# Hybrid layer (HGRN2 beside MLA): rope step of the MLA queries cut in three and pinned in the engines' orders; token-sum tiles laid in another order

## The chip, the cores and the metric

The kernel runs on one core of one Trainium2 chip. A core has a matrix engine (TensorE, PE in the profile), VectorE (DVE), ScalarE (ACT), GpSimd (POOL) and SyncE (SP). Each engine carries out its own instructions in order and waits for the others through semaphores. ACT, POOL and SP also issue DMA transfers; an issue stands in the engine's order like any other instruction. The metric is the time of one execution on the device in microseconds (us), the median of several runs; lower is better.

## The reference

One decoder layer for 512 tokens of width 1024, in float32. A normed input h is projected to all the columns that two branches and their gates need:

```
h    = rms_norm(x);  proj = h @ w_in
hq, hf, hi, hz, cq, ckv, kr, mz, glog = split(proj)
y_a  = HGRN2(hq, hf, hi) per head, normed, * silu(hz)     # 8 heads of 128, a gated linear recurrence in chunks of 32
q    = rms_norm(cq) @ w_uq                                # 8 heads of 128 + 64
q_pe = rope(q[..., 128:])                                 # the 64 rope columns of each head
kv   = rms_norm(ckv) @ w_ukv;  k_pe = rope(kr)            # one rope key for all heads
y_b  = causal softmax((q_nope k_nope + q_pe k_pe) * scale) @ v, * silu(mz)
m    = sigmoid(g_a) * (y_a @ w_proj_a) + sigmoid(g_b) * (y_b @ w_proj_b)
out  = rms_norm(x + m @ w_out)
```

The change touches how and when `q_pe` is made, and where some operands of the gates' products lie in memory.

## The kernel before

Every large matrix product is done as three products of rounded parts (high by high, high by low, low by high): `mm3`, L91 to L93. The parts of the weights are made on the fly: ACT casts the high part `w_hi` (L118), DVE subtracts to get the low part `w_lo` (L119). The accumulators of projections lie in three PSUM slots called `mm_ps`; a slot is free for PE again when whoever reads it is done.

The program has four stages: the norm and the low-rank projections (to about 55 us), HGRN2 in four pairs of heads (`hg_pair`, to about 290 us), the eight MLA heads (to about 425 us), and the gates' and the output's products, in the manner of Strassen.

In `hg_pair` the order is: forget projection and `hg_forget` for two heads (ACT: tanh, L454; DVE: f L455, scan L459, reciprocal L460, then products; POOL: L456, L457, small products, and at the end k64, L477), then for odd pairs the gate (ACT L562, DVE L563, `z`), the query projection and `hg_query` (ACT L485, POOL L489 and others), `hg_states` (PE transposes L498, ACT copy kt L499, PE products L503), scores, and `hg_out` with its norm (ACT L547, POOL L165 and L166). Pair 3 is the last, and around it the first MLA head is started: `mla_turn(0)` stands in the program before pair 3, `mla_rope` and `mla_nope(0)` after its states.

The rope for a pair of MLA heads: `mla_turn` makes the rope columns of q by a small product, ACT copies them (L626), four DMAs issued by ACT swap the halves of each head (L628), POOL multiplies by the two tables and adds (L629 to L631, each 128x512), and two more DMAs issued by ACT swap the two heads (L635, 128 KB each). `mla_rope` then has ACT round the swapped part (qh, L641) and copy each head's own rows (qp, L644), and DVE subtract for the other rows (L645).

An MLA head has scores (`mla_scores`: PE, L691 being the rope part; DVE; ACT exp L697; POOL scaling of p, L699), then a gate, the next head's q and k (`mla_nope`, whose parts qn and kn are made by ACT L160 and DVE L161), the previous head's output, and the transposes of p (L715).

Where one engine's order isn't written out by hand, the scheduler orders an engine's instructions as it estimates that they are ready. `tc.issue_after(x)` pins instructions behind x in their own engine's order. `last_pool` holds the last computing instruction of a step on POOL; `step()` has POOL issue two adding DMAs (L758) behind it, one pair after each stage of a pair or head, to build weight sums in DRAM.

Tiles of a `Pool` are laid out by the order of allocation. After the MLA heads the pool `h_sums` takes tiles s1 to s4, into which POOL loads sums of the tokens (L949) that the gates' products use.

Of the kernel before, what the change touches and what calls it, by code (L numbers as in the profile page):

```python
# [9 lines left out]
F32 = mybir.dt.float32  # L10
F32R = mybir.dt.float32r
U8 = mybir.dt.uint8
BF16 = mybir.dt.bfloat16
AF = mybir.ActivationFunctionType
ALU = mybir.AluOpType
# [3 lines left out]
P = 128  # L19
D = 1024  # L20
S = 512
NT = S // P
KD = D // P
H = 8
# [8 lines left out]
SCALE = (128 + 64) ** -0.5  # L33
# [5 lines left out]
def hybrid_layer(ctx: ExitStack, tc: tile.TileContext, a):  # L39
    nc = tc.nc  # L40
# [19 lines left out]
    def z_tile():  # L60
        return zpool.tile([P, S], F32, tag="z", name="z")
# [91 lines left out]
            for t in range(2):  # L153
                done(2 * t2 + t, ps[t])

    last_pool = [None]

    def split(hi, lo, src):

# [268 lines left out]
    ma_pool = Pool("mla_a", "right")  # L428
    qtab = ma_pool.tile([P, 2, S], F32, "qtab")
# [5 lines left out]
    for i in range(2):  # L435
        gh = hw.tile([P, NT, 12], F32, f"gh{i}")
# [7 lines left out]
    c4 = lambda t: t[:].rearrange("p (g n c) -> p g n c", n=4, c=C)  # L444
    c2_ = lambda t: t[:].rearrange("p (g n c) -> p g n c", n=2, c=C)

    def bc(gh, o, n):
        return gh[:, :, o : o + n].rearrange("p g (n o) -> p g n o", o=1).broadcast_to([P, NT, n, C])
# [32 lines left out]
    def hg_query(h, pq, pr):  # L481

        gh = gh_[h % 2]
        q = W("f", 1)
        nc.scalar.activation(q[:], pq[:], AF.Tanh, scale=0.5)  # L485
        nc.vector.scalar_tensor_tensor(q[:], q[:], 1.0, pq[:], op0=ALU.add, op1=ALU.mult)
        qi, q128, q64 = W("qi"), W("q128"), W("q64", 2, (P, S // 2))
        nc.vector.tensor_tensor(qi[:], q[:], pr[:], op=ALU.mult)
        last_pool[0] = nc.gpsimd.tensor_tensor(c2_(q64), c4(qi)[:, :, 2:4], bc(gh, 10, 2), op=ALU.mult)  # L489
        nc.vector.tensor_tensor(c4(q128), c4(qi), bc(gh, 4, 4), op=ALU.mult)  # L490
        return qi, q64, q128

    def hg_states(h, k128, ft, v_sb):
# [70 lines left out]

    v_sb = [None] * NT

    def hg_pair(pair, before_gate=None, last=None):
        cc, hs = pair * 256, (2 * pair, 2 * pair + 1)
        pf = proj_ch(w_in, COL_F + cc, hT)
        kk = [hg_forget(h, pf[i]) for i, h in enumerate(hs)]  # L570
        if pair:
            step()
        else:
            early_sums(kh[0])
        def gate():
            pz = proj_ch(w_in, COL_ZA + cc, hT)
            zz = [z_tile() for _ in hs]
            for i in range(2):
                silu2(zz[i][:], pz[i][:])
            return zz  # L580

        if pair % 2 == 0:
            for t in range(NT):
                v_sb[t] = hw.tile([P, 512], F32, f"v{t}")
            proj_tok(w_in, COL_I + cc, hT, lambda t, ps: nc.scalar.copy(v_sb[t][:], ps[:]))
        else:
            zz = gate()
        pq = proj_ch(w_in, COL_Q + cc, hT)
        qq = [hg_query(h, pq[i], kk[i][0]) for i, h in enumerate(hs)]
        step()  # L590
        sts = [hg_states(h, kk[i][5], kk[i][1], v_sb) for i, h in enumerate(hs)]
        if before_gate:
            before_gate()
        if pair % 2 == 0:
            zz = gate()
        def scores():
            return hg_scores([(h, kk[i][2:5] + qq[i][0:2]) for i, h in enumerate(hs)])

        def outs(aa):
            on = [hg_out(h, aa[i], sts[i], qq[i][2], v_sb) for i, h in enumerate(hs)]  # L600
            step()
            return on

        def gated(on):
            for i, h in enumerate(hs):
                hg_gate(h, on[i], zz[i])

        if last:
            return last(scores, outs, gated)
        gated(outs(scores()))  # L610
# [11 lines left out]
    def mla_turn(pair):  # L622

        ps = low(load_w(w_uq[:, :, 2 * pair : 2 * pair + 2, 128:192]), 0, 3)
        qr, qs = ma_pool.tile([P, S], F32, "qr"), ma_pool.tile([P, S], F32, "qs")
        nc.scalar.copy(qr[:], ps[:])  # L626
        for b in range(4):
            nc.scalar.dma_start(qs[32 * b : 32 * b + 32, :], qr[32 * (b ^ 1) : 32 * (b ^ 1) + 32, :])  # L628
        nc.gpsimd.tensor_tensor(qr[:], qr[:], qtab[:, 0], op=ALU.mult)  # L629
        nc.gpsimd.tensor_tensor(qs[:], qs[:], qtab[:, 1], op=ALU.mult)  # L630
        nc.gpsimd.tensor_tensor(qr[:], qr[:], qs[:], op=ALU.add)  # L631

        qx = ma_pool.tile([P, S], F32, "qs")
        for i in range(2):
            nc.scalar.dma_start(qx[64 * i : 64 * i + 64, :], qr[64 - 64 * i : 128 - 64 * i, :])  # L635
        return qr, qx

    def mla_rope(qr, qx):

        qp, qh = [ma_pool.tile([P, S], F32R, f"qp{i}") for i in range(2)], ma_pool.tile([P, S], F32R, "qh")  # L640
        nc.scalar.copy(qh[:], qx[:])  # L641
        for i in range(2):
            own, other = slice(64 * i, 64 * i + 64), slice(64 - 64 * i, 128 - 64 * i)
            nc.scalar.copy(qp[i][own], qr[own])  # L644
            nc.vector.tensor_tensor(qp[i][other], qx[other], qh[other].bitcast(F32), op=ALU.subtract)  # L645
        return qp

    def mla_values(h0):
# [32 lines left out]
    def mla_scores(h, pool, qn, kn, qp, final=False):  # L681

        pn = []
        for i in range(NT):
            n = (i + 1) * P
            bl = slice(i * P, n)
            sps = ax_tile()
            qh = qp[h % 2]
            mm3(sps[:, :n], qn, kn, (slice(None), bl), (slice(None), slice(0, n)), True, False)
            for x in range(2):  # L690
                nc.tensor.matmul(sps[:, :n], qh[:, bl], kpe[x][:, :n], start=False, stop=x == 1)  # L691
            sm = pool.tile([P, 4], F32, "sm", 4)
            p = pool.tile([P, n], F32, f"p{i}")
            nc.vector.tensor_tensor(sps[:, bl], sps[:, bl], mask_inf[:], op=ALU.add)
            nc.vector.tensor_reduce(sm[:, 0:1], sps[:, :n], axis=AX.X, op=ALU.max, negate=True)
            nc.vector.tensor_scalar(sm[:, 1:2], sm[:, 0:1], SCALE, None, op0=ALU.mult)  # L696
            nc.scalar.activation(p[:, :n], sps[:, :n], AF.Exp, scale=SCALE, bias=sm[:, 1:2], accum_out=sm[:, 2:3])  # L697
            nc.vector.reciprocal(sm[:, 3:4], sm[:, 2:3])
            scaled_p = (nc.vector if final else nc.gpsimd).tensor_scalar(p[:, :n], p[:, :n], sm[:, 3:4], 0.5,  # L699
                                                                         op0=ALU.mult, op1=ALU.mult)  # L700
            if not final:
                last_pool[0] = scaled_p
            pn.append(p)
        return pn
# [98 lines left out]
    def step():  # L803
        if adds and last_pool[0]:
            x = adds.pop(0)
            if x:
                x[0].add(x[1])
# [20 lines left out]
            gated(on)  # L828
        return z

    turned_q = mla_turn(0)
    z = hg_pair(H // 2 - 1, first_scores, last_outputs)
    hw.close()

    def a_parts(src, to):
# [70 lines left out]
    yb = ybp.tile([P, H, S], F32, "yb")  # L906
    qp, nope, pn = early
    late = None
    for h in range(H):
        pools = (ma_pool, mw)  # L910
        if h % 2 and h + 1 < H:
            turned_q = mla_turn((h + 1) // 2)
        if h:
            pn = mla_scores(h, pools[h % 2], *nope, qp, h + 1 == H)
        if h % 2 and h + 1 < H:
            qp = mla_rope(*turned_q)
        if h:
            z = mla_gate(h)
        if h:
            if h + 1 < H:  # L920
                nope = mla_nope(h + 1, pools[(h + 1) % 2])
            mla_out(*late)
            if h % 4 == 0:
                v = mla_values(h)
        hook = lambda: mla_transpose(pn)
        if h + 1 == H:
            with tc.manual_schedule(engines={mybir.EngineType.PE}):
                pts, later = [], []
                w11, w21 = gate_w[0].block(0, 0), gate_w[0].block(1, 0)
                u = ch_product(w11, h11, copied("c11", 1.0))  # L930
                ch_product(w21, h12, lambda b, ps: later.append((b, ps)), tile=mm_tile, hook=lambda: pts.extend(hook()))
                mla_out(h, pts, v, z)
        elif h:
            late = (h, hook(), v, z)
            step()
        else:
            with tc.manual_schedule(engines={mybir.EngineType.PE}):
                nope = mla_nope(1, pools[1])
                v = mla_values(0)
                late = (0, hook(), v, z)  # L940
    mw.close()
    ma_pool.close()
    cpool.close()

    hs = Pool("h_sums", "right")
    s1, s2, s3, s4 = [[hs.tile([P, 4, 256], F32R, f"s{n}{i}") for i in range(2)] for n in range(1, 5)]
    for n, s in ((1, s1), (2, s2), (4, s4), (3, s3)):
        for i in range(2):
            nc.gpsimd.dma_start(s[i][:], h_dram[n - 1][i][:])  # L949
# [82 lines left out]
    s1, s2 = [[sp.tile([P, 4, 256], F32R, f"s{n}{i}") for i in range(2)] for n in (1, 2)]  # L1032
# [173 lines left out]
```

## Time and profile before

| | us |
|---|---|
| median of 3 runs (lowest to highest) | 622.16 (621.46 to 623.14) |
| the profiled execution, its own time | 623.33 |
| its span | 621.4 |
| PE busy in the span | 604.7 (97%) |
| DVE, ACT, POOL busy | 431.7, 285.2, 147.6 |

The rows are read so: in an order of time, the first two numbers are start and duration in us, then engine, line, operation, result and operands, and in brackets how long the engine stood idle before it and who ended that. In a list by line, "min/median/max" are durations in ns. In a window row the numbers are the length, PE's busy time with its count of products, the granted TensorE clock (1.00 is full), the DMA engines' busy share and GB/s.

### The profile page before, as it was taken

How to read it: one execution, taken by the hardware profiler on the slowest of the kernel's cores; microseconds unless marked ns; L12 is line 12 of the kernel's file. 1: busy time of each engine (PE TensorE's matmuls, PEld its weight loads, DVE VectorE, ACT ScalarE, POOL GpSimd, SP SyncE). 2: the span in 40 equal slices, each digit the busy share in tenths (PEclk: the TensorE clock that was granted, in tenths of full speed). 3: DMA queues.
4: the chain of work that ended last, by engine and by line, in shares of the span. 5: the costliest groups of instructions: out<-in, count | busy, mean ns of one | idle time of the engine just before them, and what ended most of it. 6: DMA issues, size and time to landing. Idle time of an engine off the chain costs nothing.

```text
span 621.4 us, 9796 instructions
## 1 busy us (share of the span) xinstructions
PE 604.7 (97%) x3688; PEld 528.3 (85%) x3688; DVE 431.7 (69%) x679; ACT 285.2 (46%) x531; POOL 147.6 (24%) x245
## 2 busy tenths in 40 slices
PE   8999999999999998999998999999999999999995
PEld 5998888888888886788887888799999999888884
DVE  7727989499864538948564864766865787676796
ACT  5645244323243342335553555446667764323452
POOL 3106322444350155411525223320000000000002
PEclk9999999999999998999999999999999999999998
DMA  8449479987979946572466577496656556595213
GB/s 272 142 143 334 156 225 374 289 213 166 286 130 297 246 131 126 115 142 70 98 127 140 120 164 174 86 326 196 191 186 202 181 172 193 184 339 188 69 34 136
DMA packets 74800, 114.37 MB, mean 184 GB/s; under 512 B 7513, under 2 KB 41727, under 8 KB 74753
## 3 DMA queue, kind: packets, MB, share of 16 engines
q1 hardware_dynamic: 65100, 89.69, 44.8%
q0 software_dynamic: 7952, 21.50, 19.2%
q10 hardware_dynamic: 1700, 2.56, 1.4%
q8 instruction: 29, 0.48, 0.3%
q14 instruction: 19, 0.15, 0.1%
HBM read 105.34 MB, written 39.85 MB: 234 GB/s over the span
## 4 chain that ended last, share of the span: by engine, by line
PE 69%; DVE 10%; DMA 8%; ACT 5%; issue 4%; POOL 2%; ACTq 1%; POOLq 0%; SPq 0%; DVEq 0%
PE ax_ps L849 16%; PE mm_ps L91 13%; PE mm_ps L92 13%; PE mm_ps L93 13%; PE mm_ps L849 3%; DVE w_lo L119 3%; DMA w_raw<-w_proj_b 2%; DMA w_raw<-w_uq 2%; ACT w_hi L118 2%; PE mm_ps L271 2%; DMA qs<-qr 1%; DMA w_raw<-out_t 1%; DMA w_raw<-w_out 1%; DVE ya L1077 1%; PE ax_ps L691 1%
## 5 line engine op out<-in xcount | busy, mean ns | idle before, releaser
L119 DVE TENSOR_TENSOR w_lo<-w_raw,w_hi 128x1024 fp32r<-128x1024 f32 (+3 forms) x116 | 136.7, 1190 | 98.5 <-ACT w_hi L118 92.8
L118 ACT CAST w_hi<-w_raw 128x1024 fp32r<-128x1024 f32 (+3 forms) x116 | 114.8, 1004 | 147.4 <-PE mm_ps L92 65.1
L91 PE MATMUL mm_ps<-hT,w_hi 128*128 128x512 f32 x320 | 126.3, 396 | 2.8 <-DVE z L563 2.0
L92 PE MATMUL mm_ps<-hT,w_hi 128*128 128x512 f32 x320 | 125.7, 393 | 0.0
L93 PE MATMUL mm_ps<-hT,w_lo 128*128 128x512 f32 x320 | 125.5, 394 | 0.0
L91 PEld LDWEIGHTS mm_ps<-hT,w_hi 128*128 128x128 f32 x320 | 60.6, 189 | 15.7 <-DVE z L563 2.4
L93 PEld LDWEIGHTS mm_ps<-hT,w_lo 128*128 128x128 f32 x320 | 60.5, 189 | 12.6
L92 PEld LDWEIGHTS mm_ps<-hT,w_hi 128*128 128x128 f32 x320 | 60.5, 189 | 11.9
L849 PE MATMUL ax_ps<-s,w_hi 128*128 128x256 f32 x384 | 54.1, 283 | 0.2 <-ACT w_hi L118 0.2
L849 PEld LDWEIGHTS ax_ps<-s,w_hi 128*128 128x128 f32 x384 | 49.6, 192 | 0.5 <-ACT w_hi L118 0.5
L1094 POOL TENSOR_SCALAR ssum<-ssum 128x1 f32<-128x1 f32 x3 | 0.9, 310 | 183.9 <-ACT sq L1081 183.9
L93 PE MATMUL mm_ps<-w_hi,hT 128*128 128x512 f32 (+1 forms) x96 | 36.6, 383 | 0.0
L92 PE MATMUL mm_ps<-w_lo,hT 128*128 128x512 f32 (+1 forms) x96 | 36.5, 382 | 0.0
L91 PE MATMUL mm_ps<-w_hi,hT 128*128 128x512 f32 (+1 forms) x96 | 36.4, 386 | 0.0
L849 PE MATMUL ax_ps<-s,w_lo 128*128 128x256 f32 x192 | 31.3, 284 | 0.2 <-DVE w_lo L119 0.2
L699 POOL TENSOR_SCALAR p<-p,sm 128x128 f32<-128x128 f32 (+3 forms) x28 | 15.8, 568 | 63.5 <-DVE sm L696 52.7
L697 ACT ACTIVATE p<-ax_ps,sm 128x128 f32<-128x128 f32 (+3 forms) x32 | 16.9, 530 | 26.1 <-DVE sm L696 23.9
L849 PEld LDWEIGHTS ax_ps<-s,w_lo 128*128 128x128 f32 x192 | 26.6, 192 | 0.4 <-DVE w_lo L119 0.4
L460 DVE RECIPROCAL tf<-pr 128x512 f32<-128x512 f32 x8 | 26.8, 3346 | 0.1
L457 POOL TENSOR_SCALAR k<-tf,c1n,c 128x512 f32<-128x512 f32 x8 | 16.0, 1995 | 26.6 <-ACT tf L454 26.6
L91 PE MATMUL mm_ps<-cT,w_hi 128*128 128x512 f32 x52 | 20.7, 398 | 0.0
L93 PEld LDWEIGHTS mm_ps<-w_hi,hT 128*128 128x128 f32 x96 | 18.0, 188 | 3.0
(298 smaller groups left out, 1210.9 us busy)
## 6 DMA issues: line engine op xcount, KB each, us to landing
w_raw<-w_in SPq DMA_DIRECT2D x54, 512.0 KB, 6.5
g_t<-w_in SPq DMA_DIRECT2D x16, 512.0 KB, 8.8
w_raw<-g_t SPq DMA_DIRECT2D x16, 512.0 KB, 4.8
g_t<-w_in POOLq DMA_DIRECT2D x8, 512.0 KB, 10.9
pa_t<-w_proj_a SPq DMA_DIRECT2D x8, 512.0 KB, 13.2
g_t<-g_t POOLq DMA_DIRECT2D x8, 512.0 KB, 11.3
out_t<-w_out SPq DMA_DIRECT2D x8, 512.0 KB, 8.8
s<-h POOLq DMA_DIRECT2D x8, 512.0 KB, 7.6
```

The source lines that it names most:

```text
L91: nc.tensor.matmul(ps, lh[lsl], rh[rsl], start=start, stop=False)
L92: nc.tensor.matmul(ps, lh[lsl], rl[rsl], start=False, stop=False)
L93: nc.tensor.matmul(ps, ll[lsl], rh[rsl], start=False, stop=stop)
L118: last_hi[0] = nc.scalar.copy(hi[:, :o], raw[:, :o])
L119: last_lo[0] = nc.vector.tensor_tensor(lo[:, :o], raw[:, :o], hi[:, :o].bitcast(F32), op=ALU.subtract)
L271: nc.tensor.matmul(ps, hT[l][:, 4 * kh + k, t * P : t * P + P], c_hl[kh][r][:, k * 256 : k * 256 + 256], start=kh == 0 and kind == 0 and k ...
L457: nc.gpsimd.tensor_scalar(k[:], tf[:], c1n[:, h : h + 1], c1[:, h : h + 1], op0=ALU.mult, op1=ALU.add)
L460: nc.vector.reciprocal(rp[:], pr[:])
L691: nc.tensor.matmul(sps[:, :n], qh[:, bl], kpe[x][:, :n], start=False, stop=x == 1)
L697: nc.scalar.activation(p[:, :n], sps[:, :n], AF.Exp, scale=SCALE, bias=sm[:, 1:2], accum_out=sm[:, 2:3])
L699: scaled_p = (nc.vector if final else nc.gpsimd).tensor_scalar(p[:, :n], p[:, :n], sm[:, 3:4], 0.5, op0=ALU.mult, op1=ALU.mult)
L849: nc.tensor.matmul(ps[:, o], w[k // 2][i][:, k % 2, cols], ap[j][:, k], start=not banks and c == 0 and n == 0, stop=n == 11, skip_group_ch ...
```

## The change

Three pieces take the place of two. `mla_turn` ends after the four half swaps. A new `mla_rotate` has the three POOL operations (now L636 to L638) and the two swaps of heads, which POOL now issues (L641); all of it is pinned behind `last_pool`, and becomes `last_pool` itself, so that a following `step()` comes after it. `mla_rope` (ACT L649 and L652, DVE L653) is pinned behind `last_act` and `last_dve`, which are set in `hg_query` and `mla_scores`. For pair 0 the rotation is called after pair 3's forget steps, `mla_rope` stays after its states. `mla_turn(1)` moves from head 1 to before head 0; the turns for pairs 2 and 3 go from heads 3 and 5 to heads 2 and 4, and the rotations follow heads 0, 2 and 4. In the pool `h_sums`, s3 is now laid first, then s1, s2, s4; the loads are issued in the order they had.

```diff
-    last_pool = [None]
+    last_pool, last_dve, last_act = [None], [None], [None]
...
-        nc.scalar.activation(q[:], pq[:], AF.Tanh, scale=0.5)
+        last_act[0] = nc.scalar.activation(q[:], pq[:], AF.Tanh, scale=0.5)
...
-        nc.vector.tensor_tensor(c4(q128), c4(qi), bc(gh, 4, 4), op=ALU.mult)
+        last_dve[0] = nc.vector.tensor_tensor(c4(q128), c4(qi), bc(gh, 4, 4), op=ALU.mult)
...
-    def hg_pair(pair, before_gate=None, last=None):
+    def hg_pair(pair, after_forget=None, before_gate=None, last=None):
...
         kk = [hg_forget(h, pf[i]) for i, h in enumerate(hs)]
+        if after_forget:
+            after_forget()
         if pair:
             step()
...
             nc.scalar.dma_start(qs[32 * b : 32 * b + 32, :], qr[32 * (b ^ 1) : 32 * (b ^ 1) + 32, :])
-        nc.gpsimd.tensor_tensor(qr[:], qr[:], qtab[:, 0], op=ALU.mult)
-        nc.gpsimd.tensor_tensor(qs[:], qs[:], qtab[:, 1], op=ALU.mult)
-        nc.gpsimd.tensor_tensor(qr[:], qr[:], qs[:], op=ALU.add)
-
-        qx = ma_pool.tile([P, S], F32, "qs")
-        for i in range(2):
-            nc.scalar.dma_start(qx[64 * i : 64 * i + 64, :], qr[64 - 64 * i : 128 - 64 * i, :])
+        return qr, qs
+
+    def mla_rotate(qr, qs):
+
+        with tc.issue_after(last_pool[0].ins):
+            nc.gpsimd.tensor_tensor(qr[:], qr[:], qtab[:, 0], op=ALU.mult)
+            nc.gpsimd.tensor_tensor(qs[:], qs[:], qtab[:, 1], op=ALU.mult)
+            nc.gpsimd.tensor_tensor(qr[:], qr[:], qs[:], op=ALU.add)
+            qx = ma_pool.tile([P, S], F32, "qs")
+            for i in range(2):
+                turn = nc.gpsimd.dma_start(qx[64 * i : 64 * i + 64, :], qr[64 - 64 * i : 128 - 64 * i, :])
+        last_pool[0] = turn
         return qr, qx
...
-        nc.scalar.copy(qh[:], qx[:])
-        for i in range(2):
-            own, other = slice(64 * i, 64 * i + 64), slice(64 - 64 * i, 128 - 64 * i)
-            nc.scalar.copy(qp[i][own], qr[own])
-            nc.vector.tensor_tensor(qp[i][other], qx[other], qh[other].bitcast(F32), op=ALU.subtract)
+        with tc.issue_after(last_act[0].ins), tc.issue_after(last_dve[0].ins):
+            nc.scalar.copy(qh[:], qx[:])
+            for i in range(2):
+                own, other = slice(64 * i, 64 * i + 64), slice(64 - 64 * i, 128 - 64 * i)
+                nc.scalar.copy(qp[i][own], qr[own])
+                nc.vector.tensor_tensor(qp[i][other], qx[other], qh[other].bitcast(F32), op=ALU.subtract)
         return qp
...
-            nc.scalar.activation(p[:, :n], sps[:, :n], AF.Exp, scale=SCALE, bias=sm[:, 1:2], accum_out=sm[:, 2:3])
-            nc.vector.reciprocal(sm[:, 3:4], sm[:, 2:3])
+            last_act[0] = nc.scalar.activation(p[:, :n], sps[:, :n], AF.Exp, scale=SCALE, bias=sm[:, 1:2], accum_out=sm[:, 2:3])
+            last_dve[0] = nc.vector.reciprocal(sm[:, 3:4], sm[:, 2:3])
...
-    turned_q = mla_turn(0)
-    z = hg_pair(H // 2 - 1, first_scores, last_outputs)
+    turned_q = list(mla_turn(0))
+
+    def rotate():
+        turned_q[:] = mla_rotate(*turned_q)
+
+    z = hg_pair(H // 2 - 1, rotate, first_scores, last_outputs)
...
+    turned_q = mla_turn(1)
     for h in range(H):
         pools = (ma_pool, mw)
-        if h % 2 and h + 1 < H:
-            turned_q = mla_turn((h + 1) // 2)
+        if h in (2, 4):
+            turned_q = mla_turn(h // 2 + 1)
...
             late = (h, hook(), v, z)
+            if h in (2, 4):
+                turned_q = mla_rotate(*turned_q)
             step()
...
+            turned_q = mla_rotate(*turned_q)
...
-    s1, s2, s3, s4 = [[hs.tile([P, 4, 256], F32R, f"s{n}{i}") for i in range(2)] for n in range(1, 5)]
+    s3, s1, s2, s4 = [[hs.tile([P, 4, 256], F32R, f"s{n}{i}") for i in range(2)] for n in (3, 1, 2, 4)]
```

How this moves instructions is shown at three places. The first is ACT in the forget part of pair 3, before (tf is the tanh of each of the two heads, qp and qh belong to the rope, the DMA is the swap of heads):

```order
L118 CAST w_hi<-w_raw 128x1024
L635 DMA qs<-qr 64x512 x2
L454 ACTIVATE tf<-mm_ps 128x512
L644 CAST qp_2574<-qr 64x512
L644 CAST qp_2575<-qr 64x512
L118 CAST w_hi<-w_raw 128x1024
L641 CAST qh<-qs 128x512
L118 CAST w_hi<-w_raw 128x640
L562 ACTIVATE z<-mm_ps 128x512
L454 ACTIVATE tf<-mm_ps 128x512
```

and now:

```order
L118 CAST w_hi<-w_raw 128x1024
L454 ACTIVATE tf<-mm_ps 128x512
L118 CAST w_hi<-w_raw 128x1024
L118 CAST w_hi<-w_raw 128x640
L454 ACTIVATE tf<-mm_ps 128x512
L562 ACTIVATE z<-mm_ps 128x512
```

The swap and the three rope casts have left this part, and the second tanh stands ahead of the gate's.

The second place is ACT at the states of pair 3, from the query's tanh (f) of the second head to the second head's kt; qn and kn are parts of MLA head 0. Before:

```order
L485 ACTIVATE f<-mm_ps 128x512
L499 COPY kt<-ax_ps 128x384
L160 CAST qn_2599<-mm_ps 128x512
L118 CAST w_hi<-w_raw 128x384
L160 CAST kn_2610<-mm_ps 128x512
L499 COPY kt<-ax_ps 128x384
```

and now:

```order
L485 ACTIVATE f<-mm_ps 128x512
L652 CAST qp_2574<-qr 64x512
L652 CAST qp_2575<-qr 64x512
L499 COPY kt<-ax_ps 128x384
L160 CAST qn_2599<-mm_ps 128x512
L118 CAST w_hi<-w_raw 128x1024
L160 CAST kn_2610<-mm_ps 128x512
L649 CAST qh<-qs 128x512
L499 COPY kt<-ax_ps 128x384
```

The rope casts stand ahead of the first kt, qh ahead of the second.

The third place is POOL in the same pair, from the second head's last key product (k) to the query products (q); g_t and pa_t are weight sums in DRAM, the numbers are those of buffers. Before:

```order
L477 TENSOR_TENSOR k_2385<-ko,gh_643 128x256
L758 DMA g_t_654<-g_t_652 128x1024 x2
L489 TENSOR_TENSOR q_2531<-qi,gh_639 128x256
L489 TENSOR_TENSOR q_2540<-qi,gh_643 128x256
L758 DMA pa_t_657<-w_proj_a 128x2x512 x2
```

and now:

```order
L477 TENSOR_TENSOR k_2379<-ko,gh_643 128x256
L636 TENSOR_TENSOR qr<-qr,qtab 128x512
L637 TENSOR_TENSOR qs<-qs,qtab 128x512
L638 TENSOR_TENSOR qr<-qr,qs 128x512
L489 TENSOR_TENSOR q_2531<-qi,gh_639 128x256
L641 DMA qs<-qr 64x512 x2
L766 DMA g_t_654<-g_t_652 128x1024 x2
L489 TENSOR_TENSOR q_2540<-qi,gh_643 128x256
L766 DMA pa_t_657<-w_proj_a 128x2x512 x2
```

Rotation and swap stand behind the last key product; before, the rotation stood ahead of the whole forget part.

## Prediction

> **What bounds the kernel now.** I read the page's head, then what TensorE (PE) waits for between 210 and 430 us (the only stretch in which the change moves work), then the windows and the order of time around each wait.
>
> ```profile
> span 621.4 us, 9796 instructions
> PE 604.7 (97%) x3688; PEld 528.3 (85%) x3688; DVE 431.7 (69%) x679; ACT 285.2 (46%) x531; POOL 147.6 (24%) x245
> ```
>
> PE is busy 604.7 of 621.4 us and the change takes no product away. It can only gain where PE stands still or runs at a lower clock. PE's waits from 210 to 430 us (us in total, times, longest):
>
> ```profile
> PE ax_ps L715 <- POOL p L699: 2.1, 2, 1.4
> PE mm_ps L91 <- DVE z L563: 2.0, 1, 2.0
> PE ax_ps L91 <- DVE pt L161: 1.0, 1, 1.0
> PE mm_ps L91 <- DVE qn L161: 0.8, 2, 0.5
> PE ax_ps L503 <- ACT kt L499: 0.6, 1, 0.6
> ```
>
> So 6.5 us in all is to be had, and what the clock loses behind a wait. The longest wait is in pair 3 (PE in order of time; then PE's busy time, the granted clock PEclk, DMA share and GB/s by windows):
>
> ```profile
> 244.25 0.50 PE L91 MATMUL mm_ps<-hT,w_hi 128*128 128x512 f32 x1 [1.99 <-DVE z L563]
> ...
> 245.06 0.40 PE L91 MATMUL mm_ps<-hT,w_hi 128*128 128x512 f32 x1
> 245.29 0.55 PE L92 MATMUL mm_ps<-hT,w_hi 128*128 128x512 f32 x1
> ...
> 248.62 0.48 PE L91 MATMUL mm_ps<-hT,w_hi 128*128 128x512 f32 x1
> ...
> 256.90 0.49 PE L498 MATMUL ax_ps<-ident,k 128*128 128x128 f32 x3
> ...
> 262.47 0.94 PE L503 MATMUL ax_ps<-v,kt 128*128 128x128 f32 x6 [0.62 <-ACT kt L499]
> ```
>
> ```profile
> 246.00:248.00 2.00, 2.00 (x6) 0.50 0.09 26
> ```
>
> ```profile
> 100.00:216.00 116.00, 116.00 (x769) 1.00 0.93 242
> 322.00:355.00 33.00, 30.58 (x159) 1.00 0.64 129
> ```
>
> A little over a microsecond after the 1.99 us wait the granted clock is 0.50: the eight products that start from 245.29 up to 248.62 take 3.33 us, where at the 0.23 before them (245.06 to 245.29) they would take 1.8. The wait costs 1.99 + 1.5 = 3.5 us. Pairs 1 and 2, which have the same forget steps and no rope beside them, run from 100 to 216 us without a pause.
>
> Why PE waits there: ScalarE (ACT), VectorE (DVE) and GpSimd (POOL) in order of time.
>
> ```profile
> 229.13 1.51 ACTq L635 DMA_DIRECT2D qs<-qr  x2
> 230.70 0.60 ACT L454 ACTIVATE tf<-mm_ps 128x512 f32<-128x512 f32 x1 [4.78 <-PE mm_ps L93]
> ...
> 243.69 0.60 ACT L454 ACTIVATE tf<-mm_ps 128x512 f32<-128x512 f32 x1 [3.51 <-DVE ki L475]
> ```
>
> ```profile
> 234.79 1.84 DVE L645 TENSOR_TENSOR qp<-qs,qh 64x512 fp32r<-64x512 f32 x2
> 236.56 1.21 DVE L459 TENSOR_TENSOR_SCAN pr<-f,fr 128x512 f32<-128x512 f32 x1
> ```
>
> ```profile
> 227.83 1.27 POOL L631 TENSOR_TENSOR qr<-qr,qs 128x512 f32<-128x512 f32 x1
> ```
>
> POOL's rope addition ends at 229.10. Until then the swap's two DMA issues sit at the head of ACT's queue, with the forget step's tanh (L454) behind them. On DVE the two rope subtractions end only at 236.63, and the scan of the same forget step follows at once. So scan, reciprocal, gate z, and the accumulator that z frees for PE, are all late.
>
> **Part 1: rope of pair 0 leaves pair 3's forget part.** ACT issue, rope casts and DVE subtractions move behind the query step. What is left is pair 1's order, which has no pause; I take the 3.5 us as gone. Next in line is nothing that the profile of pairs 1 and 2 shows. PE then reaches the transposes of the states (L498) at 256.90 - 3.5 = 253.4, and the second head's states product (L503), ready at 262.47 - 0.62 = 261.85, at 258.35.
>
> **Part 2: a new wait at the states.** ACT's new order there is: two rope casts qp (which wait for POOL's addition), kt of the first head, qn, a weight cast, kn, qh (which waits for the swap to land), kt of the second head. Behind qh, then, stands the copy that the second L503 needs. When does the swap land? The template is pair 1, ACT, POOL and PE:
>
> ```profile
> 120.35 0.60 ACT L454 ACTIVATE tf<-mm_ps 128x512 f32<-128x512 f32 x1 [1.34 <-PE mm_ps L93]
> ```
>
> ```profile
> 122.56 1.69 POOL L457 TENSOR_SCALAR k<-tf,c1n,c 128x512 f32<-128x512 f32 x1
> ...
> 144.11 1.13 POOL L477 TENSOR_TENSOR k<-ko,gh 128x256 f32<-128x256 f32 x1 [5.11 <-DVE ko L476]
> ```
>
> ```profile
> 145.58 0.49 PE L498 MATMUL ax_ps<-ident,k 128*128 128x128 f32 x3
> ```
>
> And the costs, by tile and line (min/median/max ns), the landing of the eight POOL loads of L949, and the ACT queue's swaps (KB, us to landing):
>
> ```profile
> L630 POOL TENSOR_TENSOR qs<-qs,qtab x4: 1283/1446/2277, 225.3 to 380.4; 128x512 f32<-128x512 f32 x4
> L641 ACT CAST qh<-qs x4: 621/622/623, 233.7 to 386.5; 128x512 fp32r<-128x512 f32 x4
> ```
>
> ```profile
> L629 POOL TENSOR_TENSOR qr<-qr,qtab x4: 1292/1292/1962, 224.0 to 378.5; 128x512 f32<-128x512 f32 x4
> L631 POOL TENSOR_TENSOR qr<-qr,qs x4: 1269/1278/1297, 227.8 to 381.8; 128x512 f32<-128x512 f32 x4
> L644 ACT CAST qp<-qr x8: 607/617/621, 231.2 to 384.9; 64x512 fp32r<-64x512 f32 x8
> ```
>
> ```profile
> L499 ACT COPY kt<-ax_ps x8: 469/476/482, 82.9 to 261.9; 128x384 f32<-128x384 f32 x8
> ```
>
> ```profile
> L949 POOL DMA_DIRECT2D s<-h x8: 557/569/614, 406.7 to 410.4; - x8
> DMA to landing us min/median/max: 3.9/7.6/11.1
> ```
>
> ```profile
> qs<-qr ACTq DMA_DIRECT2D x8, 128.0 KB, 2.4
> ```
>
> ```profile
> 261.23 0.62 POOL L489 TENSOR_TENSOR q<-qi,gh 128x256 f32<-128x256 f32 x1 [2.49 <-DVE qi L488]
> ```
>
> In pair 1 the second head's k64 (L477), behind which the rotation is pinned, ends at 145.24, 0.34 before L498; placed against 253.4 that is 253.1. In pair 1, POOL starts L457 2.2 us after the tanh, since it issues adding DMAs just then; the changed order runs 16 more products (16 x 0.23 = 3.6 us) between the sums of squares, with those issues, and the tanh. I take 1.6 of the 2.2 back: 251.45. Rotation 1.29 + 1.28 + 1.28 = 3.85 (the middle L630 row gives 0.16 more): 255.3. One product for q64 (0.62) is queued ahead of the issues: 255.9. The first issue takes 0.57, the second begins at 256.5. Landing lies between the ACT queue's 2.4 for the same 128 KB and POOL's least 3.9 for four times as much; I take 3.5, as the size speaks for the low end and the queue for the high one: 260.0. Then qh 0.62 and kt 0.48: 261.1, where before it was 262.47. That is 1.37 sooner, though PE was ready 3.5 sooner: a pause of 2.75 us. Since 1.99 us brought a half clock, I charge the same 1.5 us again (an upper end: smaller products stand there; the lower end is 0). Net of parts 1 and 2: -1.37 + 1.5 = **+0.1**. Each microsecond of landing, called L, moves the end by one.
>
> How early can it be? Even with the swap there at once, ACT ends the second kt not before: rotation 255.3, two qp 1.24 (256.5), kt 0.48 (257.0), then the rows that stand between (weights, and qn and kn, each of the duration of kn):
>
> ```profile
> 256.92 1.05 ACT L118 CAST w_hi<-w_raw 128x1024 fp32r<-128x1024 f32 x1 [1.94 <-PE mm_ps L92]
> ...
> 261.13 0.58 ACT L160 CAST kn<-mm_ps 128x512 fp32r<-128x512 f32 x1
> ```
>
> 257.0 + 0.58 + 1.05 + 0.58 + 0.62 + 0.48 = 260.3; so L below 2.7 brings nothing more, and the bound is 0.8 better than my value.
>
> **Part 3: MLA heads.** Before, POOL's rope steps (the L630 of 2.28 among them) stand between the scalings of p in heads 1, 3 and 5, and ACT's issue of the swap ahead of casts. In head 3 (ACT, then PE):
>
> ```profile
> 339.52 1.25 ACT L644 CAST qp<-qr 64x512 fp32r<-64x512 f32 x2 [4.59 <-POOL p L699]
> ```
>
> ```profile
> 338.91 0.55 PE L715 MATMUL ax_ps<-ident,p 128*128 128x128 f32 x3 [1.35 <-POOL p L699]
> ```
>
> After, rotation and issues follow the last scaling of an even head, and POOL has until the next head's scores for them; ACT's casts follow the last exp. So the 2.1 (L715 for p) and the 0.8 (qn) go; one wait of the size of the latter's, 0.4, I leave standing, since in head 1 qh and both qp now stand ahead of kn's split on ACT. Sum: 2.1 + 0.8 - 0.4 = **-2.5**. The clock in 322 to 355 is 1.00 in spite of pauses up to 1.35, so nothing is gained there from it. The 1.0 for pt is untouched.
>
> **Part 4, at nothing:** turn(1) moves ahead of head 0, nine products in another place; its four DMA issues stand among the norms of pair 3, with some us of room before the gate's transposes. The order of the s tiles matters only to when their loads may start; these begin at 406.7, and no wait on s is among PE's waits up to 430; if that cover goes, a late s costs at most what it is late.
>
> **Sum.** +0.1 - 2.5 = -2.4. The profiled execution took 623.33 (span 621.4 and 1.9 around), 1.2 above the median of 622.16; I apply the difference to the median: 619.8. A change of 0.3% is 1.87 us, the least that I count as faster (below 620.29) or slower (above 624.03).
>
> The Trainium skill, "TensorE: Matmul & The Clock Gate", section "What's actually happening", has the array fall to half clock after at least one idle window of about 3.4 us. By it no pause here would cost clock; the trace differs, since 1.99 us of waiting had 0.50 behind it. By the rule the sum would be 1.5 lower.
>
> **Rivals.**
> *The clock stays up at the new pause.* For it: pauses of 1.35 in head 3 had no drop; the one at 244 is the only case, and it may have taken the pause together with something else. Then parts 1 and 2 give -1.4: 618.3, and 617.5 with the swap at the bound. Chance 0.14.
>
> *The rotation is slow or late.* POOL's L629 and L630 took up to 1.96 and 2.28 in the rows, 1.7 more together, and the 1.6 that I took off pair 1's template may not be there. Either makes everything behind later: -2.4 + 1.7 = -0.7, 621.5. Against it: DVE has fewer steps beside POOL there. Chance 0.20.
>
> *The swap lands late, and the kernel is slower.* POOL's queue issues the adding DMAs of 512 KB too, and its eight loads of L949 took 3.9 to 11.1 us to land. Place: qh, and behind it kt and the second L503. The total is L - 5.9 against before, so from L = 7.7 it is slower than 624.03, just above the median row of 7.6; at 11.1 it would be 627.4, in the middle 625.7. Against it: these eight were issued together and share the queues, and 128 KB is a quarter. Chance 0.13.
> The Trainium skill, "SBUF — State Buffer", warns in 'The "DVE blocks DMA" trap' that a transfer issued by GpSimd starves for descriptors while VectorE runs certain copies. That speaks against this change; no run here shows it.
>
> *The moves change nothing that counts* (another step of the forget part holds PE as long): 622. Pairs 1 and 2 speak against it. Chance 0.03.
>
> **How the numbers follow.** The forecast itself has 0.50: 619.8, and with L from 2.7 to 4.7 it runs from 619.0 to 621.0; two thirds of that (0.34) lie below 620.29. Faster: 0.34 + 0.14 = 0.48; same: 0.16 + 0.20 + 0.03 = 0.39; slower: 0.13. The range goes from 617.2, just under the clock rival's best, to 623.6, over the slow rotation and a swap of some 7 us; about 0.05 lies below and 0.13 above.
>
> **What would show it.** Right: no PE wait for z near 244 and clock 1.00 from 240 to 256; a PE wait of 2 to 3.5 us before the second L503 of pair 3, released by kt, with the clock at 0.5 behind it; no PE wait for p in head 3. Wrong: if tanh and reciprocal of pair 3 are no sooner; if POOL's swap lands in over 5 us; if a pause appears in an even head, behind POOL's rotation; if the second L503 does not wait.

## The result, and the profile after

The changed kernel takes 619.95 us (median of 7 runs, 619.13 to 620.04), the kernel before in the same sessions 623.14 (7 runs, 621.46 to 625.42). The ratio is 0.9942, with a 95% interval of 0.9923 to 0.9961, that is some 3.6 us, 2.4 to 4.8. The profiled execution took 619.97 with a span of 618.2, where before had 621.4: 3.2 us less. The forecast was 619.8. Two executions far above all others (2434 us in experiment 4, 853 us in experiment 6) are left out of the figures below.

What PE waits for between 210 and 430 us in the changed kernel (total, times, longest), to be held against the five rows of before:

```profile
PE ax_ps L503 <- ACT kt L499: 3.7, 2, 3.3
```

Every wait of before but one is gone, the 1.0 for pt too, and the one that had been the smallest of the five, for kt, has grown from 0.6 to 3.7. In order of time, PE around the states of pair 3:

```profile
252.93 0.49 PE L498 MATMUL ax_ps<-ident,k 128*128 128x128 f32 x3
...
257.27 0.94 PE L503 MATMUL ax_ps<-v,kt 128*128 128x128 f32 x6 [0.39 <-ACT kt L499]
...
261.80 1.65 PE L503 MATMUL ax_ps<-v,kt 128*128 128x128 f32 x6 [3.27 <-ACT kt L499]
263.38 1.98 PE L517 MATMUL ax_ps<-qi,ki 128*64 128x64 f32 x32
...
268.01 0.50 PE L91 MATMUL mm_ps<-hT,w_hi 128*128 128x512 f32 x1
```

and the same place before:

```profile
263.34 1.15 PE L517 MATMUL ax_ps<-qi,ki 128*64 128x64 f32 x32
...
266.12 0.50 PE L91 MATMUL mm_ps<-hT,w_hi 128*128 128x512 f32 x1
```

The transposes L498 come 4.0 us sooner than before (252.93 against 256.90). The second L503 is only 0.7 ahead (261.80 against 262.47), and the projection behind the scores is 1.9 late (268.01 against 266.12): the same products take 6.21 us from the second L503 to it, where they took 3.65. The windows (length, PE busy, count, granted clock, DMA share, GB/s) show why:

```profile
260.00:262.00 2.00, 0.20 (x1) 0.73 0.90 162
262.00:264.00 2.00, 2.00 (x18) 0.50 1.05 205
264.00:266.00 2.00, 2.00 (x52) 0.50 1.05 207
266.00:268.00 2.00, 2.00 (x30) 0.56 1.11 172
```

Half clock from 261 to over 267. So the change loses 1.9 us in pair 3 and gains all that it gains later. The gates' products (by line: min/median/max ns, first and last start), before and after:

```profile
L849 PE MATMUL ax_ps<-s,w_hi x384: 278/283/384, 420.7 to 525.8; 128*128 128x256 f32 x192
```

```profile
L861 PE MATMUL ax_ps<-s,w_hi x384: 278/283/329, 416.9 to 521.7; 128*128 128x256 f32 x192
```

The first of them starts 3.8 us sooner, which makes 5.7 us between 268 and 417, in the MLA heads. Behind that 0.6 is lost again, in a last stretch whose length differs by more than that between profiled executions: from the last of these products to the end it is 95.4 us in experiment 10 and 96.7 in experiment 9, which have the same code there.

What holds kt is seen on ACT, and in front of it on POOL:

```profile
255.46 1.25 ACT L652 CAST qp<-qr 64x512 fp32r<-64x512 f32 x2 [1.30 <-POOL qr L638]
256.74 0.48 ACT L499 COPY kt<-ax_ps 128x384 f32<-128x384 f32 x1
257.11 0.59 ACT L160 CAST qn<-mm_ps 128x512 fp32r<-128x512 f32 x1
257.73 1.05 ACT L118 CAST w_hi<-w_raw 128x1024 fp32r<-128x1024 f32 x1
258.68 0.58 ACT L160 CAST kn<-mm_ps 128x512 fp32r<-128x512 f32 x1
260.75 0.62 ACT L649 CAST qh<-qs 128x512 fp32r<-128x512 f32 x1 [1.49 <-DMA qs<-qr]
261.28 0.47 ACT L499 COPY kt<-ax_ps 128x384 f32<-128x384 f32 x1
```

```profile
249.32 1.14 POOL L477 TENSOR_TENSOR k<-ko,gh 128x256 f32<-128x256 f32 x1 [5.56 <-DVE ko L476]
250.42 1.61 POOL L636 TENSOR_TENSOR qr<-qr,qtab 128x512 f32<-128x512 f32 x1
251.99 1.74 POOL L637 TENSOR_TENSOR qs<-qs,qtab 128x512 f32<-128x512 f32 x1
253.81 1.63 POOL L638 TENSOR_TENSOR qr<-qr,qs 128x512 f32<-128x512 f32 x1
255.39 1.20 POOL L489 TENSOR_TENSOR q<-qi,gh 128x256 f32<-128x256 f32 x1
256.54 1.20 POOL L641 DMA_DIRECT2D qs<-qr  x2
```

ACT is done with kn at 259.3, and the transposes that kt copies were made before that, but qh is ahead of kt in ACT's order and waits for the swap.

### The profile page after: what moved, and what is told of

Its sections match the earlier page's. It is cut to its first block, busy times and chain, and to the rows that moved or that the text cites. A ratio compares the mean times of both kernels' runs of the same rounds, so it can differ in the third digit from the quotient of the medians.

```text
span 618.2 us, 9793 instructions
## 1 busy us (share of the span) xinstructions
PE 603.2 (98%) x3688; PEld 529.1 (86%) x3688; DVE 435.7 (70%) x679; ACT 286.1 (46%) x531; POOL 151.9 (25%) x253
## 4 chain that ended last, share of the span: by engine, by line
PE 84%; DVE 8%; ACT 2%; POOL 2%; issue 2%; DMA 1%; POOLq 0%; ACTq 0%; DVEq 0%
PE mm_ps L91 17%; PE mm_ps L92 17%; PE mm_ps L93 17%; PE ax_ps L861 16%; PE mm_ps L861 3%; PE ax_ps L699 2%; PE mm_ps L271 2%; DVE w_lo L119 1%; PE ax_ps L723 1%; PE ax_ps L541 1%; DVE tf L460 1%; DVE ya L1093 1%; PE ax_ps L92 1%; PE ax_ps L93 1%; PE ax_ps L91 1%
## 5 line engine op out<-in xcount | busy, mean ns | idle before, releaser
L93 PEld LDWEIGHTS mm_ps<-w_hi,hT 128*128 128x128 f32 x96 | 18.0, 188 | 3.0
L91 PEld LDWEIGHTS mm_ps<-w_hi,hT 128*128 128x128 f32 x96 | 18.0, 188 | 3.0
```

The source lines that it names most:

```text
L91: nc.tensor.matmul(ps, lh[lsl], rh[rsl], start=start, stop=False)
L93: nc.tensor.matmul(ps, ll[lsl], rh[rsl], start=False, stop=stop)
```

## The experiments

Ten kernels, in the order in which they were run. The runs of before beside the first four had a median of 622.76, beside the next four 622.82, beside the last two 623.01.

**1. Rope behind the states.** The two records that the pins use are set by the states' last steps:

```diff
-        nc.scalar.copy(kt_[:, :n3], kps[:, :n3])
+        last_act[0] = nc.scalar.copy(kt_[:, :n3], kps[:, :n3])
...
-            nc.vector.scalar_tensor_tensor(st_[:, sl], st_[:, sp], ft[:, i : i + 1], sps[:, sl], op0=ALU.mult, op1=ALU.add)
+            last_dve[0] = nc.vector.scalar_tensor_tensor(st_[:, sl], st_[:, sp], ft[:, i : i + 1], sps[:, sl], op0=ALU.mult, op1=ALU.add)
```

> The changed kernel with the rope casts pinned behind the second copy of kt (ACT) and the last step of the states (DVE), so that no rope step stands ahead of what the states' products need; 619.95 us unedited. Theory (the wait for kt behind qh is a pause of 3.3 us and then costs 2.6 us of clock, the first wait 0.4): PE is left with a wait of some 0.6 us at the second L503, the clock stays 1.00 and the time is 614.3, 613.5 to 615.0. Rival 1 (the pause is real, the slow products behind it have another cause): 616.9. Rival 2 (another step was as late as kt, and the pause only changes its name): 619 to 620.

Measured 614.39 us (614.35 to 614.96), ratio to before 0.9869 (0.9848 to 0.9890). PE waits once, the clock stays up, and the next projection comes at 262.38 instead of 268.01:

```profile
258.73 0.94 PE L503 MATMUL ax_ps<-v,kt 128*128 128x128 f32 x6 [0.82 <-ACT kt L499]
...
262.38 0.50 PE L91 MATMUL mm_ps<-hT,w_hi 128*128 128x512 f32 x1
```

```profile
260.00:262.00 2.00, 2.00 (x70) 1.00 0.83 145
```

Both rivals fall. Where the rope's three casts and two subtractions stand in the orders of ACT and DVE was worth 5.6 us, more than the whole change.

**2. The pause filled with other work.**

```diff
-        sps, st_ = ax_tile(), W("st", 2, (P, n3))
+        sps, st_ = ax_tile(), W("st", 2, (P, n3)); [nc.tensor.matmul(sps[:], hT[0][:, 0, :P], hT[0][:, 0], start=True, stop=True) for _ in range(14 if h == H - 1 else 0)]
```

> The changed kernel with 14 extra products of 128x512 (3.2 us at full clock) put on PE ahead of the second states product, where it stood still for 3.3 us; they write into the accumulator that the real products then overwrite. Theory (the half clock from 261 to 267 us comes of the pause, and costs 2.6 us on the small products behind it): the clock stays 1.00 and the time falls to 617.4 although work was added. Rival (the products behind are slow for another reason, or the clock falls all the same): 620 or more.

Measured 617.60 us (617.48 to 618.12), 2.35 less than the changed kernel although PE does 14 products more. The scheduler also put 14 products of the scores (L517) ahead of the second L503, which is even later than there. PE goes on with its own products at 261.75, where the changed kernel did at 261.80, and the clock is 1.00:

```profile
258.39 3.43 PE L500 MATMUL ax_ps<-hT 128*128 128x512 f32 x14
261.75 0.68 PE L517 MATMUL ax_ps<-qi,ki 128*64 128x64 f32 x14
262.36 0.94 PE L503 MATMUL ax_ps<-v,kt 128*128 128x128 f32 x6
```

```profile
262.00:264.00 2.00, 2.00 (x40) 1.00 1.03 195
```

So the half clock here comes of PE standing still, and not of the other work that goes on there.

**3. The heads' part alone.** The rope of pair 0 is made as before; the edit is in how it is called (the functions ending in old are those of before, cut in two):

```diff
-    turned_q = list(mla_turn(0))
+    turned_q = list(mla_rotate_old(*mla_turn(0)))
...
-    z = hg_pair(H // 2 - 1, rotate, first_scores, last_outputs)
+    z = hg_pair(H // 2 - 1, None, first_scores, last_outputs)
...
-        early.append(mla_rope(*turned_q))
+        early.append(mla_rope_old(*turned_q))
```

> Only the heads' part: the rope of pair 0 made as before (rotation ahead of the forget part, swap issued by ACT, no pins), all the rest as changed. Theory read from the two traces (the heads gain 5.9 us, the rope of pair 0 in its new place costs 2.1): 623.1 - 5.9 = 617.2, with the pause of 2 us at 244 and its half clock back. Rival, the terms of the prediction (heads -2.5, pair 3 about 0): 620.6.

Measured 617.16 us (615.87 to 619.11), ratio 0.9917 (0.9892 to 0.9941): 5.6 us less than before. The longest of PE's waits from 210 to 430 us in its profiled execution, of 616.33 (the only others are 0.8 for kt and 0.2 for a weight):

```profile
PE mm_ps L91 <- DVE z L563: 1.7, 1, 1.7
```

The old pause is back (the clock stayed at 1.00 behind it in this execution, unlike in that of before), and there is no wait in the heads. The prediction's size for the heads, -2.5, falls.

**4. Pair 3's part alone.** The opposite: the later pairs' rope as before.

```diff
-    turned_q = mla_turn(1)
...
-        if h in (2, 4):
-            turned_q = mla_turn(h // 2 + 1)
+        if h % 2 and h + 1 < H:
+            turned_q = mla_rotate_old(*mla_turn((h + 1) // 2))
...
-            qp = mla_rope(*turned_q)
+            qp = mla_rope_old(*turned_q)
```

> Only pair 3's part: the rope of pair 0 as changed, the other pairs' rope as before (turn at heads 1, 3 and 5, swap issued by ACT, no pins). Theory read from the two traces: 623.1 + 2.1 = 625.2, no pause at 244, the one before the second L503 with half clock behind it, and the waits for p in head 3. Rival, the term of the prediction: 623.2. Rival 2 (pair 3's part is the one that pays): below 621.

Measured 626.16 us, ratio 1.0055 (1.0035 to 1.0074): 3.4 us slower than before. All of PE's waits from 210 to 430 us:

```profile
PE ax_ps L503 <- ACT kt L499: 4.2, 2, 3.6
PE ax_ps L743 <- POOL p L727: 2.4, 2, 1.4
PE ax_ps L91 <- DVE pt L161: 1.0, 1, 1.0
PE mm_ps L91 <- DVE qn L161: 0.5, 1, 0.5
```

Alone, the part that was meant to take the pause out of pair 3 costs time. The two parts, -5.6 and +3.4, make -2.2; together they gave -3.2 to -3.6. The 1 us between is within what runs differ by. This trace also has the clock fall in head 3, which neither of the two main traces has (see the clock, below); by the starts of the same products (340.60 to 344.40, against 338.91 to 341.17 before) that cost 1.5 us there.

**5. A shorter pause.** As experiment 2, with 3 products instead of 14 (`range(3 if h == H - 1 else 0)`).

> The changed kernel with 3 extra products of 128x512 ahead of the second states product, behind which the scheduler also puts 22 small products of the scores; the pause is cut from 3.3 us to about 1.9, the length of the one that before had at 244. Without a fall of the clock PE reaches the next projection 3.8 us sooner than in the changed kernel: 616.2. Theory 1 (a pause of 2 us brings half clock for 3.3 us in every run): 617.7, in a narrow range. Theory 2 (whether it does depends on where the pause falls, so it differs from run to run): runs of both kinds, from 616 to 618, as the runs of before (620.9 to 625.4) and of the heads' part alone (615.9 to 619.1) are spread, which both have such a pause. Rival (no fall below some 3 us): 616.2, narrow.

Measured 617.63 us, spread from 616.41 to 619.13. In the profiled execution, the fastest, 44 products of the scores stood ahead, not 22, so the pause was 1.25 us, shorter than the 1.9 that was meant. The clock stayed at 1.00:

```profile
261.98 0.94 PE L503 MATMUL ax_ps<-v,kt 128*128 128x128 f32 x6 [1.25 <-ACT kt L499]
```

The runs with a mean granted clock of 0.996 and 0.997 took 616.41, 616.77, 617.03 and, against the pattern, 618.32; those with 0.993 took 618.24 and 619.13. That speaks for theory 2: a short pause costs clock in some executions and not in others. Only one execution was profiled, so where the longer ones lost their clock was not seen.

**6. Tiles of the token sums as before.**

```diff
-    s3, s1, s2, s4 = [[hs.tile([P, 4, 256], F32R, f"s{n}{i}") for i in range(2)] for n in (3, 1, 2, 4)]
+    s1, s2, s3, s4 = [[hs.tile([P, 4, 256], F32R, f"s{n}{i}") for i in range(2)] for n in range(1, 5)]
```

> The changed kernel with the tiles of the token sums laid s1, s2, s3, s4 as before. Theory (the tiles only set when loads may start, and no product waits for s): 619.95, at most 0.5 from it. Rival (the loads, which start at 390.9 in the changed kernel and at 406.7 before, are needed early): later loads, a wait for s at the first token-sum product, and over 621.

Measured 619.56 us (618.57 to 621.36) against 619.95: nothing to be told from noise, and no wait for s in its trace. This edit could be left out.

**7. Turn and rotation back in the odd heads**, on the kernel of experiment 1; swap by GpSimd, pinned casts.

```diff
-        if h in (2, 4):
-            turned_q = mla_turn(h // 2 + 1)
+        if h % 2 and h + 1 < H:
+            turned_q = mla_rotate(*mla_turn((h + 1) // 2))
```

> The kernel of the first experiment (614.39) with turn and rotation of the later pairs back in heads 1, 3 and 5, swap still issued by GpSimd and the casts still pinned. Theory (the heads' gain comes from turning a head ahead, so that rotation does not stand among the scalings of p): the waits of PE for p and of the gate for qn come back, +3 to +6, 617.5 to 620. Rival (pins and the issue by GpSimd make the gain): under 616.

Measured 620.95 us (619.11 to 622.20), 6.6 more than experiment 1, and more than expected. In the profiled execution, the fastest, of 619.11, the waits for p came back, and one for pt that was not named; that for qn did not:

```profile
PE ax_ps L723 <- POOL p L707: 2.7, 2, 1.4
PE ax_ps L91 <- DVE pt L161: 0.8, 1, 0.8
```

**8. The heads' swaps issued by ACT**, on the kernel of experiment 1, behind its last exp; pair 0's still by GpSimd (`own`).

```diff
-                turn = nc.gpsimd.dma_start(qx[64 * i : 64 * i + 64, :], qr[64 - 64 * i : 128 - 64 * i, :])
+                turn = (nc.gpsimd if own else nc.scalar).dma_start(qx[64 * i : 64 * i + 64, :], qr[64 - 64 * i : 128 - 64 * i, :])
```

> The kernel of the first experiment (614.39) with the heads' swaps issued by ACT again, turns and rotations a head ahead as they are; pair 0 as it is. Theory (rotation has some 10 us of room behind the last scaling of p, so that it is of no matter who issues): 614.4, at most 0.7 from it. Rival (ACT's queue is held by the issue until GpSimd's addition ends, and the casts of p for the transposes stand behind it): a wait of 1 to 2 us per even head, 616 to 620.

Measured 614.00 us (613.68 to 614.47), ratio to before 0.9856 (0.9832 to 0.9880): not to be told from experiment 1. In the heads it does not matter which engine issues the swap, although the six issued by ACT landed later there (a median of 6.1 us after their issue, against 3.0 for GpSimd's eight in experiment 1).

**9. No pins in the heads**, on the kernel of experiment 1; pair 0 keeps its own.

```diff
-        with tc.issue_after(last_pool[0].ins):
+        with tc.issue_after(last_pool[0].ins) if pin else nullcontext():
...
-        with tc.issue_after(last_act[0].ins), tc.issue_after(last_dve[0].ins):
+        with (tc.issue_after(last_act[0].ins) if pin else ExitStack()), (tc.issue_after(last_dve[0].ins) if pin else ExitStack()):
```

> The kernel of the first experiment (614.39) without the pins of the later pairs' rope: turn a head ahead and swap by GpSimd as they are, rotation and casts where the scheduler puts them, which is again among the scalings of p in heads 0, 2 and 4. Theory (what counts is that the rotation stands behind the last scaling of a head, by whatever means): waits of PE for p come back in heads 2 and 4, +2 to +5, 616.5 to 619.5. Rival (turning a head ahead is enough, since the data are there earlier): 614 to 615.

Measured 622.01 us (620.65 to 622.69), 7.6 more than experiment 1, outside what was expected on the slow side. In the profiled execution, the fastest, of 620.65, only one wait for p came back, 1.2 us at 323. The largest, and three more of together 1.2 us, lie between 279 and 289, at the end of pair 3 and the start of the heads:

```profile
275.54 1.29 POOL L636 TENSOR_TENSOR qr<-qr,qtab 128x512 f32<-128x512 f32 x1 [3.94 <-DMA qs<-qr]
...
279.12 0.69 DVE L549 TENSOR_TENSOR k<-ax_ps,ss 128x512 f32<-128x512 f32 x1 [11.06 <-POOL ss L166]
```

```profile
279.86 0.50 PE L91 MATMUL ax_ps<-kn,qn 128*128 128x512 f32 x1 [1.27 <-DVE k L549]
```

The turn of the second pair now stands ahead of head 0, and without pins its rotation goes ahead of the last norms of pair 3 in POOL's order and waits there for its swap of halves, until 275.54; in experiment 1 those norms let DVE start L549 at 272.92. So the expected waits in heads 2 and 4 are the smaller part, and most of what was seen is a new wait that the earlier turn brings when nothing holds the rotation back. Turning a head ahead and pinning are worth their time only together: without either one, the time is 6.6 to 7.6 us longer, more than the 5.6 that the heads' part had gained.

**10. All swaps issued by ACT**, in the changed kernel.

```diff
-            nc.gpsimd.tensor_tensor(qr[:], qr[:], qs[:], op=ALU.add)
-            qx = ma_pool.tile([P, S], F32, "qs")
-            for i in range(2):
-                turn = nc.gpsimd.dma_start(qx[64 * i : 64 * i + 64, :], qr[64 - 64 * i : 128 - 64 * i, :])
-        last_pool[0] = turn
+            last_pool[0] = nc.gpsimd.tensor_tensor(qr[:], qr[:], qs[:], op=ALU.add)
+        qx = ma_pool.tile([P, S], F32, "qs")
+        for i in range(2):
+            nc.scalar.dma_start(qx[64 * i : 64 * i + 64, :], qr[64 - 64 * i : 128 - 64 * i, :])
```

> The changed kernel (619.95) with all swaps issued by ACT again, everything else as changed. In pair 3 the scheduler then puts the issue ahead of the second query tanh, kt and the weights of the first head's q and k on ACT. Theory (an engine that issues is held until the rotation ends, some 255.4 us, and all that stands behind is late): PE stands still from about 253 to 260 instead of from 258.5 to 261.8, the second L503 comes some 4.5 us later: 624.5, 622 to 627. Rival (the queue does not matter, or ACT's faster landing makes up for it): 619 to 621.

Measured 621.02 us (620.70 to 621.86), 1.1 more than the changed kernel: less than the theory's 622 to 627, and just above the rival's 619 to 621. ACT and PE in pair 3:

```profile
255.28 1.17 ACTq L641 DMA_DIRECT2D qs<-qr  x2
256.55 0.60 ACT L485 ACTIVATE f<-mm_ps 128x512 f32<-128x512 f32 x1 [5.71 <-PE mm_ps L92]
...
261.49 0.62 ACT L649 CAST qh<-qs 128x512 fp32r<-128x512 f32 x1 [1.60 <-DMA qs<-qr]
262.01 1.04 ACT L118 CAST w_hi<-w_raw 128x1024 fp32r<-128x1024 f32 x1
262.96 0.58 ACT L160 CAST kn<-mm_ps 128x512 fp32r<-128x512 f32 x1
263.44 0.48 ACT L499 COPY kt<-ax_ps 128x384 f32<-128x384 f32 x1
```

```profile
263.97 1.65 PE L503 MATMUL ax_ps<-v,kt 128*128 128x128 f32 x6 [5.13 <-ACT kt L499]
```

ACT is held until the rotation ends, as expected, but that is not what makes the second L503 late: ACT catches up and then stands idle for 1.60 us until the swap has landed. The L503 comes 2.2 us later than in the changed kernel (263.97 against 261.80), not 4.5. Of this, 0.7 is a later start of qh (261.49 against 260.75), though the swap was issued 1.3 us sooner; the other 1.4 are a weight cast and kn, which there stood ahead of qh and here stand between qh and kt. So the theory failed in its mechanism too, and ACT's faster landing, of which the rival spoke, was not seen either: all eight swaps took a median of 5.3 us.

## Why the prediction came out, point by point

The number was right by luck: two of its terms were wrong with opposite signs, and it started from a median of 622.16 (three runs), where the change was measured against 623.14; the forecast of -2.4 from there would have been 620.7.

**Part 1 held.** The pause at 244 is gone, L498 starts at 252.93 where 253.4 was worked out, and nothing else was late in its place.

**Part 2: the mechanism held, and its clock term was mis-sized.** The keys' product on POOL ended at 250.5 (251.45 worked out); the rotation took 5.0 us instead of 3.85 (1.61, 1.74 and 1.63 a step), and ended at 255.4 where 255.3 was expected, the two errors cancelling; q64 took 1.20 instead of 0.62. The swap's second issue began some 0.6 later, at about 257.1, and qh starts at 260.75, 3.6 behind it, where 3.5 was taken. Over all eight swaps:

```profile
qs<-qr POOLq DMA_DIRECT2D x8, 128.0 KB, 3.2
```

The rival of a late landing falls with this row. The second L503 began at 261.80, with 261.1 forecast, and PE had stood for 3.27, with 2.75 forecast (0.39 more at the first L503, where kt stands behind the casts that wait for POOL). The failed step is "I charge the same 1.5 us again (an upper end ...; the lower end is 0)". It was no upper end: the clock cost 6.21 - 3.65 = 2.56 us, and experiment 2 gives 2.35 for the same thing by its time alone. By the windows the half clock lasted 6.8 us here (below), where it had lasted 3.4 at 244. In experiment 4, where it lasted 3.4 at this place too, the same products took 5.19 us (262.32 to 267.51), 1.54 more than the 3.65: the 1.5 was the price of one such stretch, and here there were two. Net of parts 1 and 2: +1.9, where +0.1 stood.

**Part 3 was mis-sized the other way**: -2.5 forecast, -5.7 by the traces and -5.6 by experiment 3. Two sentences of it failed. "The 1.0 for pt is untouched" and the 0.4 left standing for qn: both waits are gone (1.4 us). And the price of a wait was taken from its bracket. PE in head 3, before, and the same ten transposes in the changed kernel:

```profile
336.15 0.27 PE L715 MATMUL ax_ps<-ident,p 128*128 128x128 f32 x1
337.12 0.44 PE L715 MATMUL ax_ps<-ident,p 128*128 128x128 f32 x2 [0.70 <-POOL p L699]
```

```profile
337.19 1.26 PE L723 MATMUL ax_ps<-ident,p 128*128 128x128 f32 x10
```

Two transposes began at 337.12 and the next only at 338.91, 1.79 later, where ten in a row take 1.26 with the last one's own end in it. The bracket of that next row says 1.35; at the row's pace of some 0.1 each about 0.2 more was lost, because a product's modelled end lies behind the time at which a next one could have started (in the run of projections at 245 us a product of 128x512 is given 0.40 us, and the next one starts 0.23 behind it). The wait at 337.12 read likewise lost 0.2 more than its 0.70. If each of the five waits in the heads (3.9 us by their brackets) did, that is 1 us more, an estimate from these two. It leaves some 0.8 of the 5.7 to no named place.

**Part 4 held**, as far as it was run: experiment 6 puts the tiles' order at nothing. The earlier place of turn(1) was not run alone: with the pins no wait of PE shows there, without them (experiment 9) there is one of 1.27 us at the end of pair 3.

**The rivals.** The clock did not stay up. The rotation was slow, as the second rival had it (1.1 of its 1.7), though it ended on time, since the keys were ready earlier. That the sum came out at -2.4, with -3.2 to -3.6 measured, is the work of errors of +1.8 and -3.2, with the 0.6 lost in the last stretch.

**The clock.** How long it stayed down is read from the windows: a window of 2 us with a granted clock of 0.73 holds 0.27 x 2 / 0.5 = 1.1 us of half clock. In the changed kernel that makes 1.1 + 2 + 2 + 1.8 = 6.8 us. In the kernel before, around the pause at 244:

```profile
244.00:246.00 2.00, 1.75 (x6) 0.84 0.79 236
...
248.00:250.00 2.00, 2.00 (x8) 0.80 0.43 98
```

with the window between them that the prediction shows, 0.6 + 2 + 0.8 = 3.4 us. The one is twice the other. Read in the same way, it lasted 10.2 us in experiment 10, behind the pause of 5.13 us (0.51 in the window from 260, 0.50 in the next four, 0.93 in the last), and 3.4 us at two places in experiment 4: at the second L503, behind a pause of 3.59 us (0.59 and 0.56 in the windows from 262 and 264), and in head 3, behind waits of 1.00 and 1.36 us for p (0.71, 0.50 and 0.93 in the windows from 340):

```profile
340.60 0.69 PE L743 MATMUL ax_ps<-ident,p 128*128 128x128 f32 x3 [1.36 <-POOL p L727]
```

```profile
342.00:344.00 2.00, 2.00 (x9) 0.50 0.71 138
```

So in these traces, the kernel's end left out, the half clock lasts one, two or three times 3.4 us, but the length of a pause alone sets neither whether it comes nor how long it stays. The same two waits for p in experiment 7 (1.38 and 1.36 us), and the pause of 1.67 us at 244 in experiment 3, had a clock of 1.00 behind them; 3.59 us brought half of what 3.27 brought. The Trainium skill, "TensorE: Matmul & The Clock Gate", section "What's actually happening", has the clock set window by window of 3.4 us that run free of the kernel; with one, two and three such windows the traces agree, and it would explain why kernels with a pause of one to two us have runs of more than one kind (experiment 5; before itself ran from 621.46 to 625.42, experiment 1, with 0.82 left, from 614.35 to 614.96). Among the 23 runs of before beside the last two experiments, the four with a mean granted clock of 0.991 or 0.992 took 624.86 to 626.49 us, the eight with 0.996 or 0.997 took 620.32 to 622.73. That a whole window must be idle is not what the rows show: 1.99 us of standing still, less than one window, was enough. What share of it must be idle stays open.

## What to carry to other kernels

When a late step is moved out of the way, ask at its new place what stands behind it in each engine's order, not only who needs its result: here a cast that nobody needed for 20 us stood ahead of a copy that the matrix engine was about to need, and putting the rope's casts behind that copy gained 5.6 us more (614.39). Price a pause of the matrix engine by the starts of its products around it, and add the clock that may fall behind it, for as long as it stays down. And when parts of a change can be run apart, do so even if the sum fits: here one part gained 5.6 us, the other lost 3.4, and the sum alone would have confirmed a wrong account of both.

## What was not expected of the hardware

The half clock came in lengths of once, twice and three times 3.4 us, and the length of the pause alone did not decide: two waits of 1.00 and 1.36 us brought it in one profiled execution, 1.38 and 1.36 us at the same place in another kernel, and 1.67 us in a third, did not. POOL's three rope steps took 1.6 to 1.7 us each in pair 3, against medians of 1.28 to 1.45 before (with single steps up to 2.28), with VectorE busy beside them; that VectorE is the reason was not tried. A transfer of 128 KB issued by GpSimd landed in 3.2 us (median of eight), against 2.4 for the same issued by ACT before; but issued by ACT in experiments 8 and 10 it took 6.1 and 5.3, so the issuing engine alone does not set it. What does was not tried.
